# Layer one's running sums and key transposes placed later, retention's transposes moved from VectorE to TensorE

## The chip, the cores and the metric

The kernel runs on one core of a Trainium2 chip. That core has five engines which follow their own instruction queues: TensorE (PE, with its weight loads shown apart as PEld), VectorE (DVE), ScalarE (ACT), GpSimd (POOL) and SyncE (SP), which here issues all transfers. The metric is the device time of one execution in microseconds (us); the time of the kernel before is the median of three runs.

## What is computed

Two transformer layers on one sequence of 1024 tokens, width 1024, all in 32-bit floats. Layer one normalizes the input, projects it, and joins a neighbourhood attention (eight heads of 64) with a gated delta rule (four heads of 128, forward and backward):

```python
aq, ak, av, az, dq, dk, dv, dz, b_f, a_f, b_b, a_b = _split_proj(proj)
attn = _neighbourhood_attention(rms(aq), rms(ak), av, rpb) * silu(az)
qkv = silu(_centred_depthwise_conv([dq, dk, dv], conv_w))       # then l2norm of dq and dk
g = -exp(a_log) * softplus(a + dt_bias)                         # gates; inside each chunk:
g = jnp.cumsum(g, axis=-1)                                      # their running sums
sol = triangular_solve(I + strict(kb k^T * decay), [v*beta, kb*exp(g)])
y = concat([attn, delta]) @ w_out;  x = x + y
```

Layer two has a stick-breaking attention (eight heads of 128) and a retention (four heads of 256) whose state runs over chunks of keys and values:

```python
qb, kb = rotary(r_q), rotary(r_k) / 16
scores = einsum('qd,kd->qk', qc, kc) * intra_decay
out    = scores @ vc + (q_c * q_decay) @ state
state  = state * chunk_decay + einsum('kd,ke->de', k_c * k_decay, v_c)
out_b  = rms_norm(ret, ret_out_gain) * silu(r_g)
```

Both branches are projected, gated, merged and projected once more.

## The kernel before

**Products.** Each matrix product of width 1024 is done to nearly full precision from two halves: an operand is split into a high part and a rest, and three of the four products are summed. `load_units` brings 128 rows of weights at a time through SP (tile `raw`, line 64) and POOL splits them into `wu` (lines 70 and 71; ten buffers of `wu`). `dense_col` (line 112) gives 128 output channels by 1024 tokens in two PSUM banks, `dense_tok` (line 102) gives 128 tokens by up to 512 channels. PSUM has eight banks: three with the tag "a", two with "z", one each with "p", "t" and "o". Retention before uses "a", "z", "t" and "o" and leaves "p" empty.

**Order.** The program is unrolled. The framework puts each engine's instructions into one fixed order when the program is built: source order is the priority, and an instruction whose inputs its planner expects to be late lets later ones pass. On the chip each engine then follows its queue in that order, so an instruction that waits holds all that stand behind it on its engine.

**Layer one, start.** After the first normalization the gates are projected (tile `gates`), and DVE and ACT work out `graw`. Two matmuls with triangles of ones (lines 285 and 286) make the running sums `gc`, a transpose (line 289) and a copy make `growt`, and SP stores it to `d_g` (line 292). All of it stands ahead of the first delta head. The tiles of this part are in a pool `gp`, which is closed after it; the pool `dc` (tiles `pad`, `cv`, `s1`, `s2`) opens on the same memory. While this runs, POOL multiplies `dzt` by a gain (line 250).

**Layer one, delta heads.** The loop `for h in range(4)` projects queries, keys and values (block `b` 0 to 2), copies each into `pad` (line 315), runs the five-step convolution on DVE (lines 318 and 320), and silu. Then for each half `g` of the tokens: transposes of the keys (341), their norms with a power on POOL (`ks`, 126), the scaled `kt` (346), transposes of the values (351), and the transposes of `kt` back (355) into `kT`. `G` is read back from `d_g`, decays are built, and `N`, `IT` and three products go to memory; SP loads the collected `N` as `X`.

**Layer one, attention.** `solver` inverts 64x64 triangles in 62 steps on DVE and POOL (lines 463 and 465). `na_proj(p)` projects a pair of attention heads, scales queries and keys (tiles `qn`, `kn`), and after every fourth block of tokens transposes four `kn` (line 514) into a bank "a", from which ACT and DVE make the two halves of `kS` (517 and 518). `na_attn` does the scores, softmax and values. The solver's steps, `na_attn(p)` and `na_proj(p + 1)` are woven together.

**Layer two, retention.** For each head `ret_proj(h)` projects queries and keys, rotates them on DVE (1095 to 1098) and POOL (1099 and 1100), and projects values (`v`, 1109) and gates. `ret_chain(h, ...)` then has two groups `g` of four chunks: scores (1143), weights `wT`; `kf`, the keys transposed by sixteen 32x32-block transposes on DVE (line 132, helper `dve_transpose`); `kd`, their two halves scaled by the decay (ACT 1154, DVE 1155); then for each chunk the output `po` (1163, 1171), its norm, the products with `kd` (1184) and the state (1190, 1194, 1195). `kd` has one buffer. At a group's end `ob` is made from the outputs `ot` by sixteen more DVE transposes (line 132), scaled (ACT 1201), gated (POOL 1202) and stored to `d_ob` (1204). `kf` and `ob` share one buffer, tag "ob": `kf` of a group can be written once `ob` of the group before it is stored. PE fills the time between the steps of a chain with the next head's `ret_proj`.

Of the kernel before, what the change touches and what calls it, by code (L numbers as in the profile page):

```python
# [11 lines left out]
F32 = mybir.dt.float32  # L12
F32R = mybir.dt.float32r
AF = mybir.ActivationFunctionType
# [13 lines left out]
def f32(ap):  # L28
    return ap.bitcast(F32)
# [7 lines left out]
def tile_kernel(ctx: ExitStack, tc: tile.TileContext, I: dict, out: bass.AP, dbg=None, stop=None):  # L37
# [49 lines left out]
    def bank(tag, w=512):  # L87
        if tag == "a":
            return psA.tile([P, w], F32, tag="a", name="acc")
        return psB.tile([P, w], F32, tag=tag, name="p" + tag, bufs=2 if tag == "z" else 1)  # L90
# [36 lines left out]

    def dve_transpose(dst, src):

        for a in range(4):  # L130
            for b in range(4):
                nc.vector.transpose(out=dst[32 * b:32 * b + 32, :, :, 32 * a:32 * a + 32],
                                    in_=src[32 * a:32 * a + 32, :, :, 32 * b:32 * b + 32])

    class Halves:
# [120 lines left out]

    gp_ = tc.tile_pool(name="gp", bufs=1)
    gp = gp_.__enter__()
    onesPP = gp.tile([P, P], F32, name="onesPP")
# [23 lines left out]
    gc = sm.tile([P, 8, NM], F32, name="gc")  # L283
    pg = bank("z")
    nc.tensor.matmul(pg[:, 0:32], lhsT=trile, rhs=graw[:, 0:4, :], start=True, stop=True)
    nc.tensor.matmul(pg[:, 32:64], lhsT=trige, rhs=graw[:, 4:8, :], start=True, stop=True)
    nc.vector.tensor_copy(out=gc, in_=pg[:, 0:64])
    pgt = bank("z")
    nc.tensor.transpose(pgt[:64, 0:P], gc.rearrange("p a b -> p (a b)"), ident)
    growt = gp.tile([64, P], F32, name="growt")  # L290
    nc.vector.tensor_copy(out=growt, in_=pgt[:64, 0:P])
    nc.sync.dma_start(out=d_g.rearrange("a (n c) -> (a n) c", n=NM), in_=growt)
    el = sm.tile([P, 8, NM], F32, name="el")
    eS = sm.tile([P, 8, NM], F32, name="eS")
    rq = sm.tile([P, 4, NM], F32, name="rq")

    gp_.__exit__(None, None, None)


    dn_ = tc.tile_pool(name="dn", bufs=1, side="right")  # L300
    dn = dn_.__enter__()
    dc_ = tc.tile_pool(name="dc", bufs=1)
    dc = dc_.__enter__()
    for h in range(4):
# [5 lines left out]
        for b in range(3):  # L310
            pad = dc.tile([P, T + 4], F32, tag="pad", name="pad", bufs=2)
            nc.gpsimd.memset(pad[:, 0:2], 0.0)
            nc.gpsimd.memset(pad[:, T + 2:T + 4], 0.0)
            for half, acc in enumerate(dense_col(hT, us, b * P)):
                nc.scalar.copy(out=pad[:, 2 + half * 512:2 + half * 512 + 512], in_=acc)  # L315
            cv = dc.tile([P, T], F32, tag="cv", name="cv", bufs=2)
            blk = b * 4 + h
            nc.vector.tensor_scalar_mul(out=cv, in0=pad[:, 0:T], scalar1=conv_w[:, blk, 0:1])
            for i in range(1, 5):
                nc.vector.scalar_tensor_tensor(out=cv, in0=pad[:, i:i + T], scalar=conv_w[:, blk, i:i + 1],  # L320
                                               in1=cv, op0=ALU.mult, op1=ALU.add)
            s = (dc if b else dn).tile([P, T], F32, tag="s%d" % b, name="s", bufs=1 if b else 2)
            nc.scalar.activation(out=s, in_=cv, func=AF.Silu)
            sT.append(s)
# [12 lines left out]
        for g in range(2):  # L337
# [11 lines left out]
            for j in range(4):  # L349
                m = g * 4 + j  # L350
                nc.tensor.transpose(pv[:, j * P:(j + 1) * P], sT[2][:, m * P:(m + 1) * P], ident)
            nc.scalar.copy(out=vt[:, g * 4:g * 4 + 4, :].rearrange("p m d -> p (m d)"), in_=pv)
            pk2 = bank("o")
            for j in range(4):
# [124 lines left out]
    def na_proj(p, hold):  # L479
# [11 lines left out]
        hold.append((qn, kS, v, z, TB))  # L491
        kns = []
        for m, acc in dense_tok(hT, us, 0, 384):
            j = m % 4
            sq = na1.tile([P, 256], F32, tag="sq", name="sq", bufs=2)
# [3 lines left out]
            rsqrt_small(ss, ss, 1.0 / 64, EPS, 4)  # L499
            kn = na1.tile([P, P], F32, tag="kn", name="kn", bufs=5)  # L500
            nc.scalar.copy(out=qn[:, m, :], in_=acc[:, 0:128])
# [6 lines left out]
            kns.append(kn)  # L508
            if j == 3:
                sl = slice((m - 3) * P, (m + 1) * P)  # L510

                pt = bank("a")
                for jj, k_ in enumerate(kns):
                    nc.tensor.transpose(pt[:, jj * P:(jj + 1) * P], k_, ident)
                for hh in range(2):
                    a, b = slice(hh * 64, hh * 64 + 64), slice(64 - hh * 64, 128 - hh * 64)
                    nc.scalar.activation(out=kS[hh][a, sl], in_=pt[a, :], func=AF.Copy, scale=gk[a])
                    nc.vector.scalar_tensor_tensor(out=kS[hh][b, sl], in0=pt[a, :], scalar=gk[a],  # L518
                                                   in1=f32(kS[hh][a, sl]), op0=ALU.mult, op1=ALU.subtract)
                kns = []  # L520
            yield 1
        for half, acc in enumerate(dense_col(hT, us, 384)):
            last_na[0] = nc.scalar.activation(out=z[:, half * 512:half * 512 + 512], in_=acc, func=AF.Silu)
        yield 1

# [545 lines left out]
    with tc.tile_pool(name="rt", bufs=1) as rt:  # L1071
# [61 lines left out]
        def ret_chain(h, tiles):  # L1133
            qTs, kTs, vs = tiles
            state = None
            for g in range(2):
# [3 lines left out]
                for j in range(4):  # L1140
                    cs = slice(j * P, (j + 1) * P)
                    for b in range(2):
# [7 lines left out]
                kd = [rt.tile([P, 4, 256], F32R, tag="kd%d" % x, name="kd") for x in range(2)]  # L1150
                kf = rt.tile([P, 4, 256], F32, tag="ob", name="kf")
                dve_transpose(kf.rearrange("p n (b c) -> p b n c", b=2), kT.rearrange("p b (n c) -> p b n c", n=4))
                kf, kh, kl = [t_.rearrange("p a b -> p (a b)") for t_ in [kf] + kd]
                nc.scalar.activation(out=kh, in_=kf, func=AF.Copy, scale=rdv[:, h, 0:1])
                nc.vector.scalar_tensor_tensor(out=kl, in0=kf, scalar=rdv[:, h, 0:1], in1=f32(kh),
                                               op0=ALU.mult, op1=ALU.subtract)
                ot = rt.tile([P, 4, 256], F32, tag="ot", name="ot")
# [38 lines left out]
                ob = rt.tile([P, 2, 4, P], F32, tag="ob", name="ob")  # L1196
                dve_transpose(ob, ot.rearrange("p n (b c) -> p b n c", b=2))
                for b in range(2):
                    ga = rt.tile([P, 512], F32, tag="ga", name="gb", bufs=2)
                    nc.sync.dma_start(out=ga, in_=d_gb[2 * h + b, :, g * 512:(g + 1) * 512])  # L1200
                    nc.scalar.activation(out=ob[:, b], in_=ob[:, b], func=AF.Copy, scale=rgn[:, 2 * h + b:2 * h + b + 1])
                    nc.gpsimd.tensor_tensor(out=ob[:, b].rearrange("p n c -> p (n c)"), in0=ob[:, b].rearrange("p n c -> p (n c)"),  # L1202
                                            in1=ga, op=ALU.mult)
                    nc.sync.dma_start(out=d_ob[2 * h + b, :, g * 512:(g + 1) * 512], in_=ob[:, b].rearrange("p n c -> p (n c)"))
# [135 lines left out]
```

## Time and profile before

| | |
|---|---|
| median of three runs | 2288.43 us (2281.90 to 2291.71) |
| the profiled execution | 2281.08 us, of which the span is 2279.4 us |
| PE busy | 2171.1 us (95%) |
| DVE busy | 1222.5 us (54%) |
| POOL busy | 1107.4 us (49%) |
| ACT busy | 763.6 us (33%) |
| mean granted TensorE clock | 0.985 of full speed |

The span runs from the first to the last instruction. Busy time is a union: pipelined matmuls overlap, and the ends shown for them are modelled, so the spacing of their starts tells their cost better than their length. A granted clock of 1.00 is 2.4 GHz, one of 0.50 is 1.2 GHz; a mean between them says which share of a stretch was spent at either. "Idle before" or a bracket behind an instruction tells how long its engine stood still ahead of it, and what ended that.

### The profile page before, as it was taken

Reading aid. Unit: us, or ns where it says so; the run is one execution under the profiler, and the core shown is the slowest. Engines: PE = TensorE matmul, PEld = TensorE weight load, DVE = VectorE, ACT = ScalarE, POOL = GpSimd, SP = SyncE. Lnnn points to the kernel's source line nnn. Section 1 sums busy time; section 2 is a strip of 40 time slices with the busy share of each in tenths; the row PEclk is TensorE's granted clock in tenths of the full one; section 3 lists DMA queues with packets and bytes.
Section 4 is the critical chain, followed back from the end, with each engine's and each line's share of the span. In section 5 each row is a group of like instructions: output and inputs, shape, how many; then the busy total and the mean of one; then the engine's idle time right before and its main releaser. Section 6 shows DMA issues by size and latency. Waiting matters only on the chain.

```text
span 2279.4 us, 33389 instructions
## 1 busy us (share of the span) xinstructions
PE 2171.1 (95%) x12197; PEld 1872.3 (82%) x12197; DVE 1222.5 (54%) x2228; ACT 763.6 (33%) x1904; POOL 1107.4 (49%) x1435
## 2 busy tenths in 40 slices
PE   7999888899999989999999999999989999999999
PEld 7777777687888878899999988888878788788887
DVE  4688789943457474556566541417474744321321
ACT  5344433445455233334344331112222222321200
POOL 6668787762003253333344442537575744444531
PEclk9999999999999999999999999999999999999999
DMA  4256830045386441111111113111333232654432
GB/s 131 85 155 163 206 109 26 36 118 165 103 301 228 148 131 47 54 33 36 56 56 52 56 61 103 37 65 56 130 112 129 84 107 93 222 171 153 148 107 102
DMA packets 238788, 249.23 MB, mean 109 GB/s; under 512 B 40032, under 2 KB 173856, under 8 KB 238368
## 3 DMA queue, kind: packets, MB, share of 16 engines
q1 hardware_dynamic: 238624, 247.10, 34.2%
q8 instruction: 96, 1.57, 0.3%
q14 instruction: 68, 0.56, 0.1%
HBM read 171.51 MB, written 75.53 MB: 108 GB/s over the span
## 4 chain that ended last, share of the span: by engine, by line
PE 54%; POOL 5%; issue 3%; DMA 2%; DVE 2%; ACT 1%; SPq 0%; POOLq 0%; ACTq 0%
PE acc L112 29%; PE acc L102 13%; PE acc L859 3%; PE po L1055 2%; PE pz L1023 2%; POOL wu L71 1%; POOL wu L70 1%; PE pt L1050 1%; PE pt L1171 1%; DMA d_oag<-oa 1%; DMA oa<-d_oa 1%; PE acc L1003 1%; POOL ob L1202 1%; PE pp L1050 0%; PE acc L120 0%
## 5 line engine op out<-in xcount | busy, mean ns | idle before, releaser
L112 PE MATMUL acc<-h2h,wu 128*128 128x512 f32 x1504 | 460.1, 396 | 0.7 <-POOL wu L71 0.4
L102 PE MATMUL acc<-wu,h2h 128*128 128x384 f32 (+1 forms) x1536 | 370.0, 324 | 6.8 <-DVE v L1109 4.0
L71 POOL TENSOR_TENSOR wu<-raw,wu 128x512 fp32r<-128x512 f32 (+3 forms) x268 | 364.1, 1367 | 7.0
L70 POOL TENSOR_SCALAR wu<-raw 128x512 fp32r<-128x512 f32 (+3 forms) x268 | 206.4, 773 | 330.1 <-PE acc L112 249.1
L112 PEld LDWEIGHTS acc<-h2h,wu 128*128 128x128 f32 x1504 | 282.1, 188 | 65.4 <-ACT lg L956 1.2
L102 PEld LDWEIGHTS acc<-wu,h2h 128*128 128x128 f32 x1536 | 268.0, 191 | 12.7 <-DVE v L1109 4.9
L112 PE MATMUL acc<-h2l,wu 128*128 128x512 f32 x752 | 278.3, 395 | 0.0
L102 PE MATMUL acc<-wu,h2l 128*128 128x384 f32 (+1 forms) x768 | 246.0, 321 | 0.0
L102 PE MATMUL acc<-wu,h1hi 128*128 128x384 f32 (+2 forms) x768 | 192.0, 333 | 12.6 <-DVE kS L518 6.7
L112 PE MATMUL acc<-h1hi,wu 128*128 128x512 f32 x512 | 165.8, 412 | 6.8 <-ACT pad L315 3.3
L125 POOL TENSOR_SCALAR ss<-ss 128x2 f32<-128x2 f32 (+2 forms) x136 | 37.1, 273 | 277.6 <-ACT sq L980 218.8
L112 PEld LDWEIGHTS acc<-h2l,wu 128*128 128x128 f32 x752 | 141.2, 188 | 31.1
L102 PEld LDWEIGHTS acc<-wu,h1hi 128*128 128x128 f32 x768 | 137.1, 195 | 17.0 <-issue 8.0
L102 PEld LDWEIGHTS acc<-wu,h2l 128*128 128x128 f32 x768 | 146.1, 190 | 1.9
L102 PE MATMUL acc<-wu,h1lo 128*128 128x384 f32 (+2 forms) x384 | 126.7, 333 | 0.0
L112 PEld LDWEIGHTS acc<-h1hi,wu 128*128 128x128 f32 x512 | 99.2, 195 | 31.7 <-ACT pad L315 4.4
L126 POOL TENSOR_TENSOR ss<-ss,mhalf 128x2 f32<-128x2 f32 (+2 forms) x136 | 119.2, 877 | 8.6
L112 PE MATMUL acc<-h1lo,wu 128*128 128x512 f32 x256 | 96.9, 407 | 0.0
L980 ACT ACTIVATE sq<-acc 128x128 f32<-128x128 f32 x128 | 35.6, 289 | 128.5 <-PE acc L102 124.4
L320 DVE SCALAR_TENSOR_TENSOR cv<-pad,c_conv_w,cv 128x1024 f32<-128x1024 f32 x48 | 76.6, 1596 | 1.1
L112 PE MATMUL acc<-oah,wu 128*128 128x512 f32 x256 | 76.9, 396 | 0.0
L1055 PE MATMUL po<-wT,v 128*128 128x512 f32 (+3 forms) x288 | 74.7, 351 | 1.7 <-DVE wT L1053 1.3
(546 smaller groups left out, 4471.5 us busy)
## 6 DMA issues: line engine op xcount, KB each, us to landing
raw<-in_w_in_dram SPq DMA_DIRECT2D x192, 256.0 KB, 2.9
d_pk<-sct SPq DMA_DIRECT2D x24, 512.0 KB, 4.3
raw<-in_w_out_dram SPq DMA_DIRECT2D x40, 256.0 KB, 2.6
wsa<-d_pk SPq DMA_DIRECT2D x16, 512.0 KB, 5.5
wsb<-d_pk SPq DMA_DIRECT2D x16, 512.0 KB, 7.6
d_sg<-lg SPq DMA_DIRECT2D x32, 256.0 KB, 2.5
sg<-d_sg SPq DMA_DIRECT2D x32, 256.0 KB, 3.6
raw<-in_w_in_dram SPq DMA_DIRECT2D x32, 192.0 KB, 2.7
```

Of the source, the lines that this page charges most:

```text
L70: nc.gpsimd.tensor_scalar(out=u[:, 0, :], in0=raw, scalar1=1.0, scalar2=0.0, op0=ALU.mult, op1=ALU.add)
L71: nc.gpsimd.tensor_tensor(out=u[:, 1, :], in0=raw, in1=f32(u[:, 0, :]), op=ALU.subtract)
L102: nc.tensor.matmul(acc[:, :n], lhsT=hT[a][:, k, m * P:(m + 1) * P], rhs=us[k][:, b, c0:c0 + n], start=(k == 0 and i == 0), stop=(k == NK - ...
L112: nc.tensor.matmul(accs[half], lhsT=us[k][:, b, c0:c0 + P], rhs=hT[a][:, k, half * 512:(half + 1) * 512], start=(k == 0 and i == 0), stop= ...
L125: nc.gpsimd.tensor_scalar(out=dst, in0=src, scalar1=mul, scalar2=eps, op0=ALU.mult, op1=ALU.add)
L126: nc.gpsimd.tensor_tensor(out=dst, in0=dst, in1=mhalf[:, :eshape], op=ALU.pow)
L320: nc.vector.scalar_tensor_tensor(out=cv, in0=pad[:, i:i + T], scalar=conv_w[:, blk, i:i + 1], in1=cv, op0=ALU.mult, op1=ALU.add)
L859: nc.tensor.matmul(acc, lhsT=us[k][:, y, (b % 4) * P:(b % 4 + 1) * P], rhs=token_set(mT[x][:, k, 0:T], s), start=(k == 0 and i == 0), stop ...
L980: nc.scalar.activation(out=sq[:, a * P:(a + 1) * P], in_=acc[:, a * P:(a + 1) * P], func=AF.Square, accum_out=ss[:, a:a + 1])
L1003: nc.tensor.matmul(acc, lhsT=us[k][:, y, 384:512], rhs=token_set(h2T[x][:, k, :], n_ // 4), start=(k == 0 and i == 0), stop=(k == NK - 1 a ...
L1023: nc.tensor.matmul(pz[:, :w], lhsT=qk[0][a][:, i * P:(i + 1) * P], rhs=qk[1][b][:, c0:c0 + w], start=(x == 0), stop=(x == 2))
L1055: nc.tensor.matmul(po[:, i0 * P:512], lhsT=v[a][:, c0 // P + kb, :], rhs=wT[b][:, :n], start=(diag and kb == 0 and x == 0), stop=(diag == ...
```

## The change

Three places in layer one and one in layer two. Layer one: the running sums become a function `cumulate`, which is called in the first head's loop after the convolution of block 0, and its tiles stay in the pool `dc`. The transposes of `kt` get a loop of their own behind both halves' other transposes. In `na_proj` the transposes of `kn` become `keys(g)`: the first half is called after block 5 in place of block 3, the second after the projection of `z`; for the first pair they use a bank "z", and `kn` has eight buffers in place of five. Layer two: `dve_transpose` goes; for each group PE transposes the keys in two lots of four 128x128 blocks into bank "p", and ACT and DVE make `kd` from there in halves; at the group's end PE transposes `ot` in two lots of four into bank "p", and ACT scales from there into `ob`. The tile `kf` is gone.

```diff
@@ start of layer one
-    gp_ = tc.tile_pool(name="gp", bufs=1)
-    gp = gp_.__enter__()
+    dc_ = tc.tile_pool(name="dc", bufs=1)
+    gp = dc = dc_.__enter__()
...
     gc = sm.tile([P, 8, NM], F32, name="gc")
-    pg = bank("z")
...
-    nc.sync.dma_start(out=d_g.rearrange("a (n c) -> (a n) c", n=NM), in_=growt)
+    def cumulate():
+        pg = bank("z")
+        nc.tensor.matmul(pg[:, 0:32], lhsT=trile, rhs=graw[:, 0:4, :], start=True, stop=True)
+        nc.tensor.matmul(pg[:, 32:64], lhsT=trige, rhs=graw[:, 4:8, :], start=True, stop=True)
+        nc.vector.tensor_copy(out=gc, in_=pg[:, 0:64])
+        pgt = bank("z")
+        nc.tensor.transpose(pgt[:64, 0:P], gc.rearrange("p a b -> p (a b)"), ident)
+        growt = gp.tile([64, P], F32, name="growt")
+        nc.vector.tensor_copy(out=growt, in_=pgt[:64, 0:P])
+        nc.sync.dma_start(out=d_g.rearrange("a (n c) -> (a n) c", n=NM), in_=growt)
...
-    gp_.__exit__(None, None, None)
...
-    dc_ = tc.tile_pool(name="dc", bufs=1)
-    dc = dc_.__enter__()
@@ delta heads, behind the convolution of a block
+            if h == 0 and b == 0:
+                cumulate()
@@ behind the transposes of the values
             nc.scalar.copy(out=vt[:, g * 4:g * 4 + 4, :].rearrange("p m d -> p (m d)"), in_=pv)
+        for g in range(2):
             pk2 = bank("o")
@@ na_proj
+        def keys(g):
+            sl = slice(g * 512, (g + 1) * 512)
+            pt = bank("a" if p else "z")
+            for jj in range(4):
+                nc.tensor.transpose(pt[:, jj * P:(jj + 1) * P], kns[g * 4 + jj], ident)
...
-            kn = na1.tile([P, P], F32, tag="kn", name="kn", bufs=5)
+            kn = na1.tile([P, P], F32, tag="kn", name="kn", bufs=8)
...
-            if j == 3:
-                sl = slice((m - 3) * P, (m + 1) * P)
-                pt = bank("a")
...
+            if m == 5:
+                keys(0)
             yield 1
         for half, acc in enumerate(dense_col(hT, us, 384)):
             last_na[0] = nc.scalar.activation(out=z[:, half * 512:half * 512 + 512], in_=acc, func=AF.Silu)
+        keys(1)
@@ ret_chain
-                kf = rt.tile([P, 4, 256], F32, tag="ob", name="kf")
-                dve_transpose(kf.rearrange("p n (b c) -> p b n c", b=2), kT.rearrange("p b (n c) -> p b n c", n=4))
-                kf, kh, kl = [t_.rearrange("p a b -> p (a b)") for t_ in [kf] + kd]
-                nc.scalar.activation(out=kh, in_=kf, func=AF.Copy, scale=rdv[:, h, 0:1])
-                nc.vector.scalar_tensor_tensor(out=kl, in0=kf, scalar=rdv[:, h, 0:1], in1=f32(kh),
-                                               op0=ALU.mult, op1=ALU.subtract)
+                for x in range(2):
+                    pk = bank("p")
+                    for j in range(2):
+                        for b in range(2):
+                            n = 2 * x + j
+                            nc.tensor.transpose(pk[:, j * 256 + b * P:j * 256 + (b + 1) * P], kT[:, b, n * P:(n + 1) * P], ident)
+                    kh, kl = [t_[:, 2 * x:2 * x + 2, :].rearrange("p a b -> p (a b)") for t_ in kd]
+                    nc.scalar.activation(out=kh, in_=pk, func=AF.Copy, scale=rdv[:, h, 0:1])
+                    nc.vector.scalar_tensor_tensor(out=kl, in0=pk, scalar=rdv[:, h, 0:1], in1=f32(kh),
+                                                   op0=ALU.mult, op1=ALU.subtract)
...
-                dve_transpose(ob, ot.rearrange("p n (b c) -> p b n c", b=2))
...
-                    nc.scalar.activation(out=ob[:, b], in_=ob[:, b], func=AF.Copy, scale=rgn[:, 2 * h + b:2 * h + b + 1])
+                    pt = bank("p")
+                    for j in range(4):
+                        nc.tensor.transpose(pt[:, j * P:(j + 1) * P], ot[:, j, b * P:(b + 1) * P], ident)
+                    nc.scalar.activation(out=ob[:, b].rearrange("p n c -> p (n c)"), in_=pt, func=AF.Copy, scale=rgn[:, 2 * h + b:2 * h + b + 1])
```

## Rows read from the trace of the kernel before

**Rows 1.** Page, busy us of each engine, share of the span, instructions.

```profile
PE 2171.1 (95%) x12197; PEld 1872.3 (82%) x12197; DVE 1222.5 (54%) x2228; ACT 763.6 (33%) x1904; POOL 1107.4 (49%) x1435
```

**Rows 2.** Windows: stretch; length; busy PE, PEld, DVE, ACT, POOL; clock; DMA; GB/s.

```profile
40.00:68.00 28.00, 25.19 (x127) 21.11 (x126) 4.22 (x10) 10.35 (x16) 16.96 (x23) 0.94 0.35 96
68.00:226.00 158.00, 147.59 (x711) 119.54 (x710) 133.41 (x117) 71.08 (x132) 117.08 (x105) 0.97 0.48 132
294.00:456.00 162.00, 140.42 (x844) 118.77 (x845) 154.29 (x344) 63.99 (x175) 132.81 (x191) 0.96 0.16 49
1460.00:1480.00 20.00, 16.08 (x98) 14.90 (x98) 15.53 (x28) 3.85 (x8) 9.20 (x8) 0.74 0.17 53
1560.00:1580.00 20.00, 16.71 (x113) 15.35 (x112) 19.27 (x26) 5.24 (x11) 19.60 (x16) 0.91 0.29 87
1670.00:1720.00 50.00, 42.11 (x303) 38.54 (x302) 33.76 (x50) 12.67 (x30) 36.68 (x36) 1.00 0.39 127
1790.00:1820.00 30.00, 24.85 (x163) 22.28 (x162) 23.85 (x35) 7.85 (x16) 28.74 (x26) 0.94 0.44 141
1430.00:1960.00 530.00, 505.77 (x2762) 433.73 (x2761) 275.73 (x459) 120.54 (x261) 295.97 (x302) 0.98 0.29 94
```

**Rows 3.** Timeline of PE, four 128x128 transposes among dense matmuls: start, length, instruction.

```profile
103.65 0.60 PE L341 MATMUL pz<-ident,s 128*128 128x128 f32 x4
104.00 0.71 PE L112 MATMUL acc<-h1hi,wu 128*128 128x512 f32 x2
104.55 0.40 PE L112 MATMUL acc<-h1lo,wu 128*128 128x512 f32 x1
104.79 0.62 PE L112 MATMUL acc<-h1hi,wu 128*128 128x512 f32 x2
105.26 0.39 PE L112 MATMUL acc<-h1lo,wu 128*128 128x512 f32 x1
```

**Rows 4.** Groups of instructions: count, busy us, mean ns, idle before and releaser.

```profile
L132 DVE STREAM_TRANSPOSE kf<-ro 32x256 f32<-32x256 f32 x128 | 55.8, 436 | 24.5 <-DMA d_ob<-ob 22.8
L132 DVE STREAM_TRANSPOSE ob<-ot 32x256 f32<-32x256 f32 x128 | 55.8, 436 | 1.9
L1190 DVE SCALAR_TENSOR_TENSOR st<-st,rdv,po 128x512 f32<-128x512 f32 x24 | 17.8, 742 | 9.2 <-PE po L1184 8.6
```

**Rows 5.** Waits of PE, 1430 to 1960 us: total us, times, longest.

```profile
PE acc L102 <- DVE v L1109: 4.0, 4, 1.7
PE pz L1143 <- POOL ro L1100: 3.2, 4, 1.2
PE po L1184 <- ACT kd L1154: 3.1, 2, 2.1
```

**Rows 6.** Timeline of PE and DVE, middle of retention's first head.

```profile
1529.53 0.76 PE L1184 MATMUL po<-v,kd 128*128 128x256 f32 x5
1557.43 7.17 DVE L132 STREAM_TRANSPOSE kf<-ro 32x256 f32<-32x256 f32 x16
1567.87 1.01 PE L1184 MATMUL po<-v,kd 128*128 128x256 f32 x3 [0.94 <-DVE kd L1155]
```

**Rows 7.** Timeline of PE and ACT, start of the delta heads.

```profile
57.65 0.41 PE L285 MATMUL pz<-graw,trile 128*128 128x32 f32 x2 [2.81 <-DVE graw L281]
66.92 1.07 ACT L315 COPY pad<-acc 128x512 f32<-128x512 f32 x2 [11.87 <-DMA d_g<-growt]
91.39 0.72 PE L112 MATMUL acc<-h1hi,wu 128*128 128x512 f32 x2 [2.11 <-POOL wu L71]
```

**Rows 8.** Timeline of PE and DVE, from the last delta head to the attention.

```profile
259.12 0.66 PE L355 MATMUL po<-ident,kt 128*128 128x128 f32 x4 [3.34 <-DVE kt L346]
294.16 0.25 DVE L463 TENSOR_TENSOR svt<-X 128x54 f32<-128x54 f32 x1 [3.05 <-DMA X<-d_N]
304.94 0.98 PE L102 MATMUL acc<-wu,h1hi 128*128 128x384 f32 x2 [4.55 <-DVE kS L518]
```

**Rows 9.** Timeline of PE, 128-column matmuls in a stretch at half clock.

```profile
1466.17 3.35 PE L1143 MATMUL pz<-ro 128*128 128x128 f32 x14 [0.47 <-POOL ro L1100]
```

More of the change, by code (lines that the diff above doesn't have):

```diff
@@ L126, in rsqrt_small @@
         nc.gpsimd.tensor_tensor(out=dst, in0=dst, in1=mhalf[:, :eshape], op=ALU.pow)
[L128 to L133, printed above, removed]
     class Halves:
@@ L283, in tile_kernel @@
     gc = sm.tile([P, 8, NM], F32, name="gc")
-    pg = bank("z")
[L285 to L291, printed above, removed]
-    nc.sync.dma_start(out=d_g.rearrange("a (n c) -> (a n) c", n=NM), in_=growt)
+    def cumulate():
[8 more added lines that the diff above has]
+        nc.sync.dma_start(out=d_g.rearrange("a (n c) -> (a n) c", n=NM), in_=growt)
     el = sm.tile([P, 8, NM], F32, name="el")
@@ L492, in na_proj @@
         kns = []
+        def keys(g):
[3 more added lines that the diff above has]
+                nc.tensor.transpose(pt[:, jj * P:(jj + 1) * P], kns[g * 4 + jj], ident)
+            for hh in range(2):
+                a, b = slice(hh * 64, hh * 64 + 64), slice(64 - hh * 64, 128 - hh * 64)
+                nc.scalar.activation(out=kS[hh][a, sl], in_=pt[a, :], func=AF.Copy, scale=gk[a])
+                nc.vector.scalar_tensor_tensor(out=kS[hh][b, sl], in0=pt[a, :], scalar=gk[a],
+                                               in1=f32(kS[hh][a, sl]), op0=ALU.mult, op1=ALU.subtract)
         for m, acc in dense_tok(hT, us, 0, 384):
-            j = m % 4
             sq = na1.tile([P, 256], F32, tag="sq", name="sq", bufs=2)
@@ L508, in na_proj @@
             kns.append(kn)
-            if j == 3:
-                sl = slice((m - 3) * P, (m + 1) * P)
-                pt = bank("a")
[L513 to L520, printed above, removed]
+            if m == 5:
+                keys(0)
             yield 1
```

## The prediction

> **What bounds the kernel now.** I read the page first, then the windows, the waits of PE and short timelines. PE is busy 95% of the span, DVE 54%, POOL 49% [rows 1], so PE's queue is the path that sets the end: a change pays where it takes idle or half-clock time from PE, and costs what it adds to PE. The windows show where PE is not full. In 68 to 226 us it is busy 147.6 of 158 us at a clock of 0.97, with DVE at 133.4. From 294 to 456 us DVE is busy 154.3 of 162 us and PE 140.4: there DVE is the bound, with the solver's steps. In retention, 1430 to 1960 us, PE is idle 24.2 us, and 20.3 us of it lie in four stretches that are 120 us long together (3.9, 3.3, 7.9 and 5.2 us); their clocks of 0.74, 0.91, 1.00 and 0.94 cost a further 5.2 + 1.8 + 0 + 1.8 = 8.8 us. The rest of retention is dense [rows 2].
>
> **Retention, what is added to PE.** Four heads, two groups, sixteen transposes each: 128. In dense work four transposes take 0.35 us to the next matmul's start, and the two matmuls behind them 0.55 us where the next three starts are 0.235 us apart: 0.35 + 0.55 - 0.47 = 0.43 us, 0.108 us each [rows 3]. 128 x 0.108 = **13.8 us**, all on the path, since PE has other work ready nearly always. The lower end is 0.35 / 4, 11.2 us. At half clock fourteen 128-column matmuls took 3.35 us, 0.24 us each [rows 9]; all 128 at that price would be 30.6 us, the upper end. I take 13.8, because most of retention stands at a clock of 1.00.
>
> The Trainium skill, page "TensorE: Matmul & The Clock Gate", section "Part 4: PE-mode transpose", speaks against the change: it gives about 275 ns for a transpose in a kernel, and says that the full clock does not engage for transposes. By its figure the added work would be an estimated 128 x 0.275 = 35 us. The rows at full clock contradict the figure for transposes among dense matmuls; whether the clock holds where they stand among idle time no row shows.
>
> **Retention, what is taken from DVE.** 256 block transposes of 0.436 us, 111.6 us, and with them a wait of 22.8 us for the store of `ob`, because `kf` shares its buffer [rows 4]. DVE's eight wide `kd` operations become sixteen of half the width out of PSUM, for which the nearest row is 0.742 us [rows 4]: 11.9 us, on an engine with room. ACT does sixteen half-width scalings for eight wide ones, and its last sixteen read PSUM; it is busy 120.5 of 530 us [rows 2], so I cost this at nothing (bare on the path, one operation more per group at DVE's 0.742 us would be 8 x 0.742 = 5.9 us).
>
> DVE is not the bound, so only what PE waits for it counts. In the first head's middle PE did the last products with the first group's `kd` at 1529.5 us and the next ones at 1567.9: 38 us later, of which `kf` took 7.2 us from 1557.4 on [rows 6]. `kf` had to wait for `ob` of the first group to be transposed, gated and stored. From PSUM, `kd` can be made as soon as the products at 1529.5 have read the old one. The stretches at 1560, 1670 and 1790 are the middles of heads 0 to 2; they hold 16.3 us of idle and 3.6 us of clock, 19.9 us. I take three quarters, 15 us: PE's waits there are for `kd`, `v` and the state, but some are for the rotation on POOL (3.2 us in all) [rows 5], which stays. In the first stretch, 1460 to 1480, the wait for `v` behind `kf` was 1.7 us [rows 5]; with a little of the clock 2.7 us. The transposes into `ob` returned nothing: PE was dense while DVE did them.
>
> New waits: bank "p" is single, so each second lot stands on PE until the first has been read, by ACT and DVE for `kd` and by ACT for `ob`, with the next head's projection queued behind it; the transposes of `ot` wait for the last norm in the same way. With 0.742 us for each reading this is bare 8 x 1.48 + 8 x 0.74 = 17.8 us; where projection work is placed between, it is nothing. I take 1.5 us, since PE's work for the next head is on hand in nearly the whole stage. **Retention: 13.8 + 1.5 - 17.7 = -2.4 us** (ends: -16 with all 29.1 us returned, +15 with none).
>
> **Layer one, start.** PE stood 2.81 us for `graw`, and the first copies into `pad` waited until 66.9 us for the store of the running sums, because `dc` opens on the memory of `gp` [rows 7]. Now PE goes on with the projection, and `pad` needs no store. The clock of 0.94 over 40 to 68 us cost 1.7 us [rows 2]. Of 2.8 + 1.7 PE may lose all again at 91.4 us, where it already waits 2.1 us for POOL's split of the next head's weights [rows 7]: I keep 1.8 us. DVE gains more. The product for the first `pad` was nearly done when the wait began at 54.8 us (57.65 - 2.81), so without both waits its copy falls near 59 us: the convolutions start some 8 us earlier, in a stage in which DVE is busy 84% of 158 us. PE's idle 10.4 us and its lost clock of 0.03 x 158 = 4.7 us in 68 to 226 are partly waits for `pad`, which DVE frees; I take 4 us of the 15 (ends 0 and 9). `cumulate` itself is unmoved work; its DVE copy now queues behind a convolution and its store behind the raw weights in SP's queue. Behind that store stand the loads of `G`, for which decays wait; the cover is the first head's own projection, and without it `G` would hold up POOL, and so the next weights, by up to the 8 us.
>
> **Layer one, keys.** The same instructions, placed later. PE waited 3.34 us for `kt` at 259 us and 4.55 us for a bank "a" held by `kS` at 304.9 [rows 8]. The second lies where DVE is the bound until 456 us: time that PE gains there it spends waiting for DVE later, so I count nothing for it (the upper end is all 4.55). What counts is when the solver starts: it stood 3.05 us for `X` at 294 us [rows 8], so it comes earlier only as the last delta head does. I take 1 us of the 3.34. **Layer one: -(1.8 + 4 + 1) = -6.8 us** (ends +1, and -4.5 - 9 - 3.3 - 4.5 = -21).
>
> **Sum:** -2.4 - 6.8 = -9.2 us. The profiled execution of 2281.1 us would become 2272; it lies 7.3 us below the median of the runs, 2288.4, for which the sum gives **2279 us**.
>
> **The rivals.**
> *The lead carries.* All 8 us of DVE's lead reach the solver, the waits for `kt` and the start add 4, and the chains become so short that the middles of the heads close: 27 of 29 us return, 13.8 + 1.5 - 27 = -12. Together -24: 2264 us. For it: the 38 us in [rows 6]. Against it: static queues rarely shift without new waits.
> *The bound engine pays (slower).* The stretches' idle time belongs to the rotation and the weight splits: POOL is busy 19.6 of 20 and 28.7 of 30 us in two of them [rows 2]. Then `kd` merely stops being the last to arrive, nothing returns, 13.8 + 1.5 = +15 stays, and layer one's lead ends at the wait for weights: 2304 us. It decides as soon as less than 8 us returns in the three middles while layer one gives nothing.
> *No effect.* Retention breaks even and DVE's bound up to 456 us takes layer one's lead: about -1, 2287 us.
> *The clock stays low for the new transposes*: all 128 run at the 1.2 GHz price of [rows 9], 30.6 in place of 13.8 us, +17 on the forecast, 2296 us. For it: 0.74 in the first stretch, where PE did 128-column matmuls between waits [rows 2, 9]. Against it: most new transposes stand in dense stretches. The Trainium skill's page named above states a rule of this kind.
>
> **How the numbers follow.** Forecast 0.45, lead carries 0.25, bound engine pays 0.13, no effect 0.12, clock 0.05. The forecast's own range, from the ends of its terms, is 2268 to 2291. Half a per cent, 11.4 us, is about what a measurement of this kernel can tell from no change. Faster by more: 0.25 and some 0.38 of the forecast's 0.45 (its lower part lies under 2277), 0.42. Slower by more: 0.12 of the bound engine's share and a little of the clock's, 0.13. Same: 0.45. The range for 8 in 10 reaches from below 2264 to near 2304: 2256 to 2301.
>
> **What would show it.** Right: PE's waits for `kd` gone, the three middles at a clock of 1.00, 128 transposes into bank "p" at about 0.11 us, the first copy into `pad` near 59 us, the solver's first step near 288 us, PE's busy time up by some 14 us and its idle time down by more. Wrong: PE waits for bank "p" or for the rotation where it waited for `kd`; a longer wait for `wu` in the second delta head; DVE as full as before from the solver's start to 456 us, with that start unmoved.

## The result, and the profile after

The changed kernel took 2271.45 us (median of 5 runs, 2268.96 to 2274.93) where the kernel before took 2284.12 us beside it: a ratio of 0.9939, 95% interval 0.9923 to 0.9955, some 14 us faster. The measured time lies in the forecast's range, 7.5 us under its 2279 us, but the two terms did not hold: layer one alone lost 5.3 us where 6.8 us of gain were forecast, and retention alone returned 14.6 us where 2.4 were.

The page of after, busy us of each engine (compare [rows 1]):

```profile
PE 2174.7 (96%) x12325; PEld 1880.4 (83%) x12325; DVE 1105.9 (49%) x1980; ACT 769.5 (34%) x1915; POOL 1088.8 (48%) x1435
```

VectorE lost 116.6 us of work and TensorE gained 3.6 us of busy time with 128 matmuls more. That 3.6 us is not their price: time at half clock counts as busy too, and retention has less of it (below). Windows of after (columns as in [rows 2]); retention begins 5.3 us later, so its first three stretches are moved along by 6 us, and the fourth is 1786 to 1806, 20 us long where it was 30:

```profile
40.00:68.00 28.00, 27.18 (x141) 22.83 (x140) 9.59 (x15) 12.49 (x18) 16.52 (x19) 1.00 0.39 111
68.00:226.00 158.00, 143.53 (x690) 116.23 (x689) 125.67 (x113) 70.36 (x131) 110.82 (x100) 0.96 0.48 133
294.00:456.00 162.00, 136.53 (x823) 114.87 (x822) 152.66 (x335) 62.84 (x170) 129.88 (x187) 0.95 0.16 50
1466.00:1486.00 20.00, 18.38 (x151) 17.90 (x151) 7.92 (x13) 4.63 (x11) 9.06 (x8) 1.00 0.18 53
1566.00:1586.00 20.00, 19.27 (x163) 19.08 (x162) 11.32 (x15) 4.15 (x12) 16.95 (x16) 1.00 0.19 56
1676.00:1726.00 50.00, 47.27 (x327) 44.13 (x326) 21.71 (x28) 12.68 (x31) 30.11 (x29) 0.97 0.36 111
1786.00:1806.00 20.00, 18.30 (x138) 17.00 (x137) 15.06 (x18) 6.05 (x13) 19.84 (x18) 1.00 0.55 169
1430.00:1960.00 530.00, 522.71 (x2953) 453.50 (x2952) 171.97 (x220) 132.43 (x281) 296.54 (x308) 1.00 0.32 102
```

In retention TensorE idles 7.3 of 530 us where it idled 24.2 [rows 2]; the first stretch now stands at a clock of 1.00 where it stood at 0.74. In layer one TensorE idles 0.8 of the first 28 us, but in 68 to 226 us TensorE idles 14.5 us where it idled 10.4.

The waits of TensorE in after, 1430 to 1960 us (total us, times, longest), where [rows 5] had `v`, the rotation and `kd`:

```profile
PE po L1186 <- DVE st L1192: 2.9, 2, 2.3
PE acc L102 <- DVE v L1107: 1.4, 3, 0.7
PE acc L102 <- POOL wu L71: 1.4, 1, 1.4
PE po L1186 <- ACT kd L1156: 0.5, 1, 0.5
```

Two rows of the same view of before, beside those of [rows 5]:

```profile
PE pt L1163 <- DVE ot L1178: 4.0, 3, 2.0
PE po L1184 <- DVE kd L1155: 2.3, 3, 1.0
```

The waits for the rotation and for `ot` are gone, those for `kd` shrank from 5.4 us (3.1 for ScalarE's half, 2.3 for VectorE's) to 0.5, and no row names bank "p". The transposes in after, timeline of TensorE:

```profile
1554.24 0.60 PE L1154 MATMUL pp<-ident,ro 128*128 128x128 f32 x4
1554.60 0.71 PE L112 MATMUL acc<-h2h,wu 128*128 128x512 f32 x2
1555.14 0.40 PE L112 MATMUL acc<-h2l,wu 128*128 128x512 f32 x1
```

They show the spacing of [rows 3]: 0.36 us to the next matmul, 0.54 for the next two, so again 0.36 + 0.54 - 0.47 = 0.43 us for four. All 64 + 64 have a length of 270 to 276 ns; none ran at half clock.

### The profile page after: what moved, and what is told of

Its sections match the earlier page's. It is cut to its first block, busy times and chain, and to the rows that moved or that the text cites. A ratio compares the mean times of both kernels' runs of the same rounds, so it can differ in the third digit from the quotient of the medians.

```text
span 2269.7 us, 33374 instructions
## 1 busy us (share of the span) xinstructions
PE 2174.7 (96%) x12325; PEld 1880.4 (83%) x12325; DVE 1105.9 (49%) x1980; ACT 769.5 (34%) x1915; POOL 1088.8 (48%) x1435
## 4 chain that ended last, share of the span: by engine, by line
PE 74%; DVE 9%; POOL 5%; DMA 4%; issue 3%; ACT 3%; SPq 1%; ACTq 0%; POOLq 0%; DVEq 0%
PE acc L112 35%; PE acc L102 18%; PE acc L857 3%; PE po L1053 2%; PE pz L1021 2%; DVE X L460 2%; DVE svt L458 2%; DMA raw<-in_w_in_dram 1%; POOL wu L70 1%; POOL wu L71 1%; PE pz L550 1%; PE pt L567 1%; PE pp L581 1%; PE pt L1173 1%; PE pt L1048 1%
## 5 line engine op out<-in xcount | busy, mean ns | idle before, releaser
L70 POOL TENSOR_SCALAR wu<-raw 128x512 fp32r<-128x512 f32 (+3 forms) x268 | 196.5, 737 | 348.6 <-PE acc L112 256.4
L112 PE MATMUL acc<-obh,wu 128*128 128x512 f32 x256 | 76.4, 395 | 0.0
```

The source lines that it names most:

```text
L70: nc.gpsimd.tensor_scalar(out=u[:, 0, :], in0=raw, scalar1=1.0, scalar2=0.0, op0=ALU.mult, op1=ALU.add)
L112: nc.tensor.matmul(accs[half], lhsT=us[k][:, b, c0:c0 + P], rhs=hT[a][:, k, half * 512:(half + 1) * 512], start=(k == 0 and i == 0), stop= ...
```

## The experiments

Each kernel is the kernel before with the edit named. A time stands beside runs of the kernel before on the same chip; us against before are worked out from the ratio. "To the end" is the time in the profiled execution from retention's first score matmul (line 1143) to the end of TensorE's last; it is 816.7 us in before and leaves layer one out. How far it scatters can be seen in the kernels that leave retention as it was (816.7 to 818.0 us) and in those with the whole retention part (801.4 to 803.5 us).

| kernel | ratio, 95% interval | us against before | to the end, us |
|---|---|---|---|
| changed kernel | 0.9939 [0.9923, 0.9955] | -13.9 | 801.8 |
| ret_only | 0.9936 [0.9916, 0.9955] | -14.6 | 803.5 |
| layer1_only | 1.0023 [1.0011, 1.0034] | +5.3 | 817.9 |
| sums_only | 1.0009 [0.9998, 1.0021] | +2.1 | 818.0 |
| keys_only | 0.9985 [0.9973, 0.9997] | -3.4 | 816.9 |
| split_only | 1.0033 [1.0020, 1.0046] | +7.5 | 817.8 |
| kf_own | 1.0091 [1.0077, 1.0105] | +20.8 | 840.3 |
| kd_pe_ob_dve | 0.9992 [0.9982, 1.0002] | -1.8 | 818.5 |
| ob_pe_kd_dve | 0.9965 [0.9953, 0.9978] | -8.0 | 808.5 |
| ret_idle_dve | 0.9951 [0.9937, 0.9964] | -11.2 | 805.1 |
| ob_dve_pe_idle | 0.9942 [0.9926, 0.9959] | -13.2 | 807.1 |
| ret_keys | 0.9913 [0.9899, 0.9927] | -19.9 | 801.4 |
| no_split | 0.9934 [0.9921, 0.9948] | -15.1 | 802.8 |

**Layer one or retention?** The two halves of the diff that stands ahead of the prediction, each alone.

> The kernel before with the whole retention part of the change and nothing else (both transposes of a block pair on TensorE). Theory A (the gain is all retention's, layer one costs some 5 us): the traces of before and after show the stretch from retention's first matmul to its last 20 us shorter (1458.92 to 1937.67 against 1464.26 to 1923.48 us), so the time is 15 to 20 us under before, 4 to 6 us under the changed kernel. Theory B (my prediction's sums): 2.4 us under before, and the rest of the gain is layer one's.

> The kernel before with everything of the change but retention. Theory A: 4 to 6 us over before, with the first head's first write to the convolution pad 6.6 us earlier (60.3 us), no gain left at the solver's start (294 us), and the second delta and attention stages 5 us late from 500 us on, as in the trace of after. Theory B (my prediction): 6.8 us under before.

2267.59 us and 2288.28 us against 2283.55. Theory A holds in the main: retention gives all of the gain and layer one costs 5.3 us, and the interval of layer one excludes even zero. A's sizes for ret_only were missed: 14.6 us in place of 15 to 20, and level with the changed kernel in place of 4 to 6 us under it. The halves alone add up to -9.3 us and together gave -13.9; with these intervals it can't be said whether they add.

**Which part of layer one?** Three kernels with one part each: the moved sums and the joined pools; the later key transposes; and this one line, ahead of the transposes of `kt`:

```diff
+        for g in range(2):
             pk2 = bank("o")
```

> The kernel before with the running sums moved behind the first head's first projection and the two pools made one; keys as before. Prediction: 5.8 us gained (1.8 of the start kept, 4 of VectorE's lead). Rival (what the trace of after shows at the solver's start, 294.05 against 294.16 us): the 6.6 us of the first stretch are eaten by waits of the second and third head, and the time is that of before within 1 us. Second rival: the later sums also move what follows the solver, and all of the 4 to 5 us that after loses in layer one are already here.

> The kernel before with only the key transposes of the attention heads placed later, one group after the sixth projection and one after the last. Prediction: no change, within 1 us. Rival: the second group now stands behind the gate projections, the scores of its four token blocks wait for it, and TensorE idles longer in the attention (a wait of 5.66 us for an output copy shows in the trace of after at 374 us, none of that size there before): 4 to 5 us over before.

> The kernel before with one edit in layer one: the transposes of kt in a loop of their own behind both halves' other transposes. Prediction: 1 us gained. Rival: the sums alone came out at a ratio of 1.0009, the keys alone at 0.9985 and all three at 1.0023, so if the parts add, this one costs 1.0029, some 6 us over before, as kT of the first half comes later and N, IT and the products with it. Second rival: the parts don't add, and this one is within 2 us of before.

The sums gave nothing, at +2.1 us within their interval of zero; the keys, costed at nothing, gave 3.4 us; the split, costed at a gain of 1 us, lost 7.5. Why the split costs that much is not shown: it changes the order of all four engines' queues (TensorE's from 108 us on), and its trace has new waits in place of old ones. That the keys would lose 4 to 5 us by a wait like the 5.66 us for `oe` in the trace of after fell: that wait is in the trace of keys_only too (6.02 us), and the kernel is faster all the same. So a wait found in one trace says little until it is priced.

What became of the sums' lead is seen in sums_only. Its first copy into `pad` comes at 60.57 us, 6.4 us early; the second head's at 98.74 us, 5.1 early; the third head's at 152.77 us, level with before. The lead is lost in between. Timeline of sums_only there, TensorE, then VectorE, then POOL:

```profile
132.71 2.07 PE L418 MATMUL pp<-s,kT 128*128 128x128 f32 x8 [3.08 <-DVE IT L422]
...
150.55 0.66 PE L352 MATMUL pt<-ident,s 128*128 128x128 f32 x4 [2.05 <-ACT s L324]
...
153.39 0.80 PE L112 MATMUL acc<-h1hi,wu 128*128 128x512 f32 x1 [1.48 <-ACT pad L314]
```

```profile
126.50 1.85 DVE L431 TENSOR_TENSOR sct<-kT,G 128x1024 f32<-128x1024 f32 x1
128.27 3.40 DVE L319 SCALAR_TENSOR_TENSOR cv<-pad,c_conv_w,cv 128x1024 f32<-128x1024 f32 x1
131.59 0.46 DVE L380 TENSOR_TENSOR el<-el,beta 128x8 f32<-128x8 f32 x1
131.98 0.68 DVE L422 TENSOR_TENSOR IT<-pp,E 128x512 f32<-128x512 f32 x1
```

```profile
127.22 3.37 POOL L431 TENSOR_TENSOR sct<-s,G 128x1024 f32<-128x1024 f32 x1
```

TensorE came to the bank "p" that `IT` is made from (line 418) while VectorE still had a convolution step of the next block ahead of `IT` in its queue, and waited 3.08 us; two waits more follow, for `s` and for `pad`. The same three are in the trace of after (3.49, 2.27 and 1.50 us at 133.0, 150.9 and 153.7 us). Together they are 6.6 us, where before has two waits of 2.8 us in this stretch:

```profile
136.63 0.50 PE L112 MATMUL acc<-h1hi,wu 128*128 128x512 f32 x1 [2.31 <-ACT pad L315]
153.01 0.65 PE L355 MATMUL po<-ident,kt 128*128 128x128 f32 x4 [0.49 <-DVE kt L346]
```

So 3.8 of the 5.1 us are seen to go in these waits; the rest is not traced.

**Is it the shared buffer?** `kf` gets a buffer of its own and nothing else changes.

```diff
-                kf = rt.tile([P, 4, 256], F32, tag="ob", name="kf")
+                kf = rt.tile([P, 4, 256], F32, tag="kf", name="kf")
```

> The kernel before with one edit: kf has a buffer of its own, so that it no longer waits for the store of ob. All transposes stay on VectorE and TensorE gets no work. Theory A (the gain of retention is the freed kd alone, whoever transposes): the 22.8 us that VectorE stood for the store are gone, TensorE's waits of 16.3 us in the three middles of the heads go too, and without the 13.8 us of transposes on TensorE the time is as low as the retention part alone or lower: 16 to 30 us under before. Theory B (kf itself is late: on VectorE it still queues behind the rotation, the norms and 7.2 us of block transposes for each of kf and ob): less than 6 us under before, with TensorE's waits for kd or for ot still in the trace.

2308.30 us, 20.8 us slower: both theories fell, A outright and B by its sign. Freed of the wait, the transposes into `kf` were put earlier in VectorE's queue. They now stand just ahead of those into `ob`, with 1.5 us of other work between, and `v` stands behind both. Timeline of kf_own, VectorE, then TensorE:

```profile
1728.73 1.34 DVE L132 STREAM_TRANSPOSE kf<-ro 32x256 f32<-32x256 f32 x3
...
1731.62 7.18 DVE L132 STREAM_TRANSPOSE ob<-ot 32x256 f32<-32x256 f32 x16
1738.83 1.09 DVE L1109 TENSOR_TENSOR v<-acc,v 128x256 fp32r<-128x256 f32 x3
```

```profile
1739.31 0.79 PE L102 MATMUL acc<-wu,h2h 128*128 128x256 f32 x2 [4.54 <-DVE v L1109]
```

For 7.18 us no `v` was taken out of its bank; TensorE filled the banks that were left and then stood 4.54 us. Its waits in 1430 to 1960 us for `v` alone grew from 4.0 [rows 5] to 16.3 us:

```profile
PE acc L102 <- DVE v L1109: 16.3, 7, 5.3
PE acc L102 <- POOL wu L71: 8.6, 6, 2.6
PE pz L1143 <- POOL ro L1099: 6.1, 3, 3.6
```

No row of this view names `kd`: the waits for it went with the shared buffer, as theory A had it, but these others came.

The Trainium skill, page "PSUM — Partial Sum Buffer", section "Engine vs sequencer instructions", says that the queues of ScalarE, VectorE and GpSimd are strictly first in, first out. The 4.54 us agree with that for VectorE.

**Which half of retention?** Of the diff in `ret_chain`, only the part that makes `kd` from bank "p", or only the part that makes `ob` from it.

> The kernel before with half of the retention part: kd is made from TensorE's transposes, ob is still transposed on VectorE. Prediction's step that the transposes into ob returned nothing: TensorE is spared 64 of its 128 transposes, 6.9 us, and nothing else changes, so the time is 6 to 8 us under the run with the whole retention part (some 22 us under before). Rival: ob's 111.6 / 2 = 56 us on VectorE hold up what the next group and the rotation need, and the work on TensorE filled idle time; the time is that of the whole retention part or above it, by up to 8 us.

> The kernel before with the other half of the retention part: ob is made from TensorE's transposes, kf is still transposed on VectorE into the buffer that it shares with ob. Theory A (the gain lies in taking ob's block transposes off VectorE): moving kd alone gave 0.9992 and both gave 0.9936, so this one gives what is left, 0.994 to 0.995, 12 to 14 us under before. Theory B (either half is enough to break up the long holds of VectorE, the second adds only its 6.9 us on TensorE): 20 us or more under before. Theory C (both are needed: kf still waits for the store of ob, and kd comes late): within 4 us of before.

`kd` alone gave 1.8 us, with zero inside its interval, and `ob` alone 8.0. The half that I had costed as worthless is worth more than the half that I had costed as the whole gain, and the two together (14.6) more than their sum (9.8). The intervals of the times are too wide for this last point, but "to the end" bears it out: against before kd_pe_ob_dve is 1.8 us longer and ob_pe_kd_dve 8.2 shorter, and the whole part 13 to 15 us shorter. Of the three theories for ob_pe_kd_dve none hit: A's 12 to 14 us is the nearest, and the interval of the run (5.0 to 10.7 us) ends just under it.

**The held queue or the chain?** The whole retention part, and VectorE does `ob`'s transposes too, into a tile that nobody reads.

```diff
+                od = rt.tile([P, 2, 4, P], F32, tag="od", name="od")
+                dve_transpose(od, ot.rearrange("p n (b c) -> p b n c", b=2))
```

> The whole retention part, and besides VectorE still transposes each group's ot by sixteen 32x32-block transposes, into a tile that nobody reads. TensorE's work and every chain of data are those of the retention part alone; only VectorE's queue is held, by some 7.2 us a group. Theory A (the loss was the held queue: v, the rotation and the norms stand behind the transposes, and TensorE behind v and the bank): the time goes up by 10 to 21 us over the retention part alone, and TensorE waits for v, ro or the split of weights behind ro. Theory B (the loss was the chain through ob to the store and to kf): no change, within 3 us of the retention part alone (ratio 0.9936 to before).

It was 3.4 us above ret_only (0.9951 against 0.9936), with intervals that overlap widely. Theory A, 10 us and more, fell; the 3 us of theory B were about met. VectorE did the whole blocks, and what stood behind them was not late:

```profile
1703.85 7.17 DVE L132 STREAM_TRANSPOSE od<-ot 32x256 f32<-32x256 f32 x16
1711.05 0.69 DVE L1149 TENSOR_TENSOR wT<-wf,wT 128x512 fp32r<-128x512 f32 x1
1711.66 0.42 DVE L1109 TENSOR_TENSOR v<-acc,v 128x256 fp32r<-128x256 f32 x1
```

So 7.2 us of held queue are not dear in themselves. They are dear where something due stands behind them, as in kf_own.

**The chain or the order?** `kd` by TensorE, `ob` by VectorE as before, and TensorE does `ob`'s 64 transposes too, unread.

```diff
                 dve_transpose(ob, ot.rearrange("p n (b c) -> p b n c", b=2))
...
+                    pt = bank("p")
+                    for j in range(4):
+                        nc.tensor.transpose(pt[:, j * P:(j + 1) * P], ot[:, j, b * P:(b + 1) * P], ident)
```

> kd from TensorE's transposes; ob, as before, from VectorE's; and TensorE also does ob's 64 transposes into bank p, where nobody reads them. So TensorE has all the work of the whole retention part, and the chain to the store of ob goes over VectorE. Theory B (the loss lies in the chain over VectorE, ScalarE and POOL to ob): the time of kd alone (ratio 0.9992) plus 6.9 us for TensorE's 64 idle transposes, 1.001 to 1.003. Theory D (the loss lies in where the fixed order puts TensorE's work between the chains, and that order follows from which engine does what): the order comes out like that of the whole retention part and so does the time, 0.993 to 0.996; if the order comes out like that of kd alone, the run doesn't tell the two apart.

64 unread transposes, 6.9 us of work for nothing on the engine that is the path, made kd_pe_ob_dve 11 us **faster**: 0.9942 against 0.9992, as fast as ret_only within the intervals. Theory B fell. By "to the end" the run is 3.6 us longer than ret_only and 11.4 us shorter than kd_pe_ob_dve, so the smaller part of the difference may still be the chain's. To see what the order did I compared the sequences of TensorE's matmuls by their lines in the traces, from 1400 us on, without the transposes:

| sequence compared with ret_only's | share in the same order | to the end, us |
|---|---|---|
| ret_keys | 99% | 801.4 |
| ret_idle_dve | 96% | 805.1 |
| ob_dve_pe_idle | 95% | 807.1 |
| ob_pe_kd_dve | 79% | 808.5 |
| before | 67% | 816.7 |
| kd_pe_ob_dve | 66% | 818.5 |
| kf_own | 65% | 840.3 |

The kernels nearest to ret_only's order are the fastest. But the share is no price: before, kd_pe_ob_dve and kf_own have about the same share and lie up to 24 us apart. The waits of TensorE in 1430 to 1960 us, first kd_pe_ob_dve, then ob_dve_pe_idle:

```profile
PE acc L102 <- POOL wu L71: 7.2, 7, 2.1
PE pt L1167 <- DVE ot L1182: 3.5, 3, 2.4
PE pz L1143 <- POOL ro L1099: 3.2, 1, 3.2
PE pz L1143 <- POOL ro L1100: 2.6, 3, 1.2
```

```profile
PE acc L102 <- POOL wu L71: 5.1, 5, 1.5
PE acc L102 <- DVE v L1109: 3.0, 3, 2.1
PE pt L1167 <- DVE ot L1182: 1.8, 2, 1.4
PE po L1188 <- DVE st L1194: 0.8, 1, 0.8
```

The scores no longer stand ahead of the rotation that feeds them (5.8 us gone), and the waits for weights and for `ot` are shorter. One more rival is that the unread work merely kept TensorE's clock up. Windows of 1430 to 1960 us, kd_pe_ob_dve and ob_dve_pe_idle:

```profile
1430.00:1960.00 530.00, 510.09 (x2828) 439.93 (x2827) 228.54 (x346) 130.53 (x279) 288.23 (x300) 0.99 0.31 100
```

```profile
1430.00:1960.00 530.00, 519.12 (x2928) 449.88 (x2927) 226.30 (x346) 131.94 (x280) 294.17 (x307) 0.99 0.31 102
```

The clock reads 0.99 in both, while the idle time fell from 19.9 to 10.9 us, so the clock is not the main part. Theory D is what the runs bear out best. The order's part is not isolated: why the order comes out so when TensorE has the transposes is not known, and no run has this order with the engines' work left as it was.

**A better kernel?** Retention with the keys, without the sums and the split; and the changed kernel without the split.

> The whole retention part and the later key transposes of the attention heads, without the moved sums and without the split of the kt loop. If the parts add (0.9936 x 0.9985): 2268 us for a before of 2283.5, 2 to 4 us under the changed kernel. If they don't: as the retention part alone.

> The changed kernel without the split of the kt loop, all else as changed. If the parts add (retention 0.9936, sums 1.0009, keys 0.9985; split 1.0033): 0.993 in one sum and 0.9939 - 0.0033 = 0.9906 in the other, that is 7 us or more under the changed kernel. Rival (the split costs only while the sums stay where they were): the time of the changed kernel, 0.9939. If it lies under 0.9913, the moved sums are worth something beside the retention and the keys, and this is the best of all.

ret_keys came out at 2265.69 us, ratio 0.9913: the best of all, 0.26% under the changed kernel's ratio, though the two intervals overlap a little. no_split came out as the changed kernel did, and the traces show why: TensorE, VectorE, ScalarE and GpSimd have the same instructions in the same order in both. Beside the sums and the keys the split changes nothing, and the two ratios are two measurements of the same queues. Layer one has that order in layer1_only too, so its +5.3 us is what the sums and the keys cost together, where alone they come to 2.1 - 3.4 = -1.3 us: the parts of layer one don't add. ret_keys and no_split differ by the sums alone, which by these two ratios cost 4.8 us (with intervals that overlap, and beside the +2.1 of sums_only).

## Why the prediction was right and wrong

**The total** came near by luck: two errors offset each other. Layer one was off by 12 us (-6.8 forecast, +5.3 alone), retention by 12 us the other way (-2.4 forecast, -14.6 alone), so that the halves alone add up to -9.3 us, almost the -9.2 forecast. The changed kernel came 7.5 us under the forecast; 4.3 us of it are the kernel before, whose median is 2284.1 us in five runs where it was 2288.4 in three. The stated range of 2268 to 2291 us is not what the ends of the terms give: -16 - 21 leads to 2251 us, +15 + 1 to 2304.

**Layer one, start.** The mechanism up to the first `pad` was right: 60.31 us in after (forecast near 59), although the sums' matmuls themselves came at 57.24 us, 0.4 us earlier than before. The step that failed is the 4 us for VectorE's lead, with the 1.8 us kept. I took TensorE's idle time in that stage for waits that an earlier `pad` shortens. The lead was gone by the third head, for the most part in waits that come in place of shorter ones in before. The solver started at 294.05 us, where 288 was forecast and before had 294.16 [rows 8]. Timeline of ScalarE and VectorE in after:

```profile
60.31 1.07 ACT L307 COPY pad<-acc 128x512 f32<-128x512 f32 x2 [5.73 <-PE acc L112]
294.05 0.26 DVE L458 TENSOR_TENSOR svt<-X 128x54 f32<-128x54 f32 x1 [2.75 <-DMA X<-d_N]
```

That "DVE as full as before from the solver's start to 456 us, with that start unmoved" would show the step wrong is what came: VectorE 152.7 of 162 us, the start unmoved.

**Layer one, keys and split.** Nothing and -1 us were forecast, -3.4 and +7.5 us measured for each alone. The step read an edit of the source as a shift of the same instructions; but the framework orders the queues anew, and the new order has its own waits.

**Retention, added work.** Right: 0.108 us each, 13.8 us, all at full clock. TensorE's busy time was a bad sign for it: 3.6 us more in place of some 14. *The clock stays low for the new transposes* did not happen. The Trainium skill's rule ("TensorE: Matmul & The Clock Gate", section "Part 4: PE-mode transpose") and its figure would have made it an estimated 35 us. The figure of about 275 ns agrees with the length of the 128 here (270 to 276 ns) but not with what each takes of TensorE's time, 0.108 us; the rule on the clock did not apply in this trace, among dense matmuls, and the clock of the first stretch even rose from 0.74 to 1.00.

**Retention, what comes back.** The term that was mis-sized: 17.7 us forecast. With 13.8 us added and 14.6 gained by ret_only, 28.4 came back, nearly all of the 29.1 us named as the end of the range. In the traces of before and after, idle time fell by 16.9 us and the clock in the four stretches costs 1.5 us (0.03 x 50) where it cost 8.8; of the 15.0 us (unrounded) by which "to the end" shrank, 13.8 - 16.9 - 7.3 = -10.4 are so accounted for. The other 4.6 us show neither as idle nor as clock. An estimate finds 3.2 us of them: a matmul's length of 0.40 us is some 0.17 us more than the spacing of starts, 0.235 us [rows 3], and counts as busy when TensorE then stands; in 1430 to 1960 us it stood 28 times in before and 9 times in after, 19 x 0.17 = 3.2. Two steps behind the term failed. "The transposes into `ob` returned nothing": `ob` alone gave 8.0 us. And that TensorE gets the middles' time back once `kd` is early. That the shared buffer made `kd` late was right, since kf_own has no wait for `kd` left; yet kf_own lost 20.8 us, with longer waits for `v` and the weights, and kd_pe_ob_dve gained 1.8 with zero in its interval: beside 6.9 us of added work its waits for weights are 7.2 us, where before has 2.5. What the runs bear out instead is that TensorE's fixed order changed; that the order alone does it is argued, not shown. The 1.5 us for bank "p" was not needed: after has no such wait (kd_pe_ob_dve has one, of 0.5 us).

**The rivals.** *The lead carries* was near on retention alone, -12 us against the -14.6 measured, but the lead in layer one that was to bring it did not carry. *The bound engine pays* and *no effect* fell with the same run. None of the rivals had the order as its mechanism.

## What to carry to other kernels

Where a framework fixes the order of each queue, price an edit by the order that it produces, and try its parts alone: an edit that only moves instructions can cost more than one that adds work, and the parts need not add. Before a gain is put down to an engine or a buffer that was relieved, put the load back unread: here VectorE's transposes of `ot`, put back unread, left 11.2 of 14.6 us standing, and 64 unread ones on TensorE brought 11 us without any further relief of VectorE, so that relief was not the main cause. A lead at the head of a stage is worth what is left of it at the stage's end, so follow one milestone from stage to stage.

## What the runs showed of the hardware

**The same instructions, 6 us apart.** Layer one has the same instructions in the same order on all four engines in before and in the six kernels that change retention alone, yet their first score matmul came between 1456.7 and 1469.0 us. Of the 9.6 us between before and ret_only 6.4 arose in the merges behind the solver. Windows of that stretch, before and ret_only (760 matmuls each), and the one long wait of TensorE in it:

```profile
518.19:611.63 93.44, 87.88 (x760) 73.37 (x760) 41.72 (x129) 50.91 (x127) 17.69 (x24) 0.96 0.40 115
```

```profile
521.17:620.98 99.81, 93.32 (x760) 78.30 (x760) 41.88 (x129) 50.88 (x127) 17.73 (x24) 0.90 0.37 109
```

```profile
540.85 0.66 PE L537 MATMUL po<-ident,qd 128*128 128x128 f32 x2 [3.06 <-DVE z L602]
```

```profile
544.82 0.66 PE L530 MATMUL po<-ident,qd 128*128 128x128 f32 x2 [4.04 <-DVE z L595]
```

A wait 1 us longer went with 20.5 us at half clock (1.2 GHz) in place of 6.8 us, and the stretch took 6.4 us more. That the longer wait brought it about is not shown. So single traces can't settle a question of 5 us here: after's trace has layer one 5.3 us late, which is of the size of this scatter, and only the medians of layer1_only settled it.

**VectorE beside POOL.** The convolution step of 3.40 us above overlaps POOL's product of 3.37 us by 2.3 us. The same step, 48 times in sums_only, takes 1.27 to 1.29 us where POOL does nothing, and 1.9 to 2.3 us where a split of weights (line 71) runs beside all of it. An instruction's length depends on what its neighbour does, so a row taken from one stage may not hold in another.
